# Cross attention: transposing the probabilities in 32x32 blocks on VectorE and moving the blocks by transfers within SBUF

## The chip, the cores and the metric

One core of a Trainium2 chip. Its engines work side by side, each through a queue of its own in order: TensorE (PE; its weight loads are shown as PEld), VectorE (DVE), ScalarE (ACT), GpSimd (POOL) and SyncE (SP), whose queue starts nearly all transfers; 16 DMA engines carry them out. The on-chip memory is SBUF (128 partitions); TensorE writes to PSUM, in banks of 128 x 512 floats. The metric is the time of one execution on the device in microseconds, as the median of the runs.

## The reference

One encoder layer over two sequences of 512 tokens of width 1024, each with a memory of 256 rows. Three branches (a state-space scan, a differential attention over the sequence, a cross attention to the memory) are gated, projected and summed, and a feed-forward block follows. All is float32. The part that the change touches is the cross attention, with 4 heads of 128:

```
def _cross_attention(q, mk, mv):
    Bn, L = q.shape[0], q.shape[1]
    s = jnp.einsum('blhd,bmhd->bhlm', q, mk).astype(jnp.float32) * (X_DH ** -0.5)
    probs = jax.nn.softmax(s, axis=-1).astype(mv.dtype)
    return jnp.einsum('bhlm,bmhd->blhd', probs, mv).reshape(Bn, L, X_WIDTH)
```

## The kernel before, in words

A matmul is made nearly exact in float32 by splitting each operand into a high part, rounded to the matmul's format, and a low part, the rest: three matmuls (high x high, high x low, low x high) for one product. The helper `split` (lines 134 and 135, or 137 and 138 with a scale) does it: ScalarE writes the high part, VectorE subtracts it from the source and writes the low part. All matmuls of the hand-ordered part go through `InOrder.matmul` and `InOrder.transpose` (lines 66 and 69), so in the profile they carry these two lines and are told apart by their tiles.

The cross attention is a loop (lines 686 to 726) over 32 steps: head h, sequence s, and a tile lt of 128 tokens, lt innermost; four steps with the same h and s are called a group here, and there are eight. For a step:

- scores: three matmuls of 128 tokens x 256 memory rows into a bank `sc`;
- softmax (`softmax_parts`, lines 541 to 550): VectorE takes the row maximum (`nb`), ScalarE the exponential `e` with the row sum, VectorE the reciprocal `r` and, on line 701, e times r;
- two steps later, TensorE transposes e in two pieces of 128x128 against the identity (line 69) into a bank `tr`, since the output matmul needs the memory rows on the partitions, and `split` brings the result from PSUM into `xpTh` and `xpTl`;
- after the fourth step of a group, six matmuls of 512 columns with the memory's values (`mvh`, `mvl`) give the outputs in a bank `oo`; ScalarE copies them to `xosb` (line 724) and SP stores them to `bD` (line 725).

TensorE's order in this part is the order of the program (`PE.on = True`); the other queues are ordered by the compiler's scheduler, with some edges given by hand (`tc.issue_after`). Between the parts of a step, `fill(n)` puts n units of other matmuls from `queue`: query projections of the next heads, gate tiles, the values of the next stage and its first projection, by `units` and `v_units`, one unit to a matmul of 512 columns. Their weights are loaded by `weight` (line 146) into a buffer `wf` of two, and split into `wh` and `wl`, of two each.

Each turn of the loop also ends in `half_piece`, which prepares weights of the last projection in the background: a load into `raw` (lines 443 and 445), sums on GpSimd (lines 452 to 455), a split into `hl` and a store to `wD` (line 472). These instructions are queued behind the last exponential (on ScalarE) and the last instruction of the softmax (on VectorE).

Two steps of scores run ahead (`AHEAD = 2`). The banks are 2 `mm` for projections, 3 `sc`, 2 `tr`, 1 `oo`. The pool `xT` has four buffers for `xpTh` and `xpTl`.

Of the kernel before, what the change touches and what calls it, by code (L numbers as in the profile page):

```python
# [10 lines left out]
F32 = mybir.dt.float32  # L11
F32R = mybir.dt.float32r
# [7 lines left out]
P = 128  # L20
L = 512
# [5 lines left out]
NMEM = 256  # L27
# [45 lines left out]
def encoder(ctx: ExitStack, tc: tile.TileContext, a, out):  # L73
    nc = tc.nc
    V, S, PO, PE = nc.vector, nc.scalar, nc.gpsimd, InOrder(tc, nc.tensor)
# [12 lines left out]
    def open_tags(es, side=None, **tags):  # L88

        for tag, n in tags.items():  # L90
            pools[tag] = es.enter_context(tc.tile_pool(name=tag, bufs=n, side=side, reuse_waits="tile"))

    def open_banks(**tags):

        bank_es.close()
        for tag, n in tags.items():
            pools[tag] = bank_es.enter_context(tc.tile_pool(name=tag, bufs=n, space=PSUM, reuse_waits="tile"))
# [4 lines left out]
    xp_es, phase = ExitStack(), ExitStack()  # L102
# [3 lines left out]
    def slot(tag, shape=(P, NT), dt=F32, name="sl"):  # L106
        return pools[tag].tile(list(shape), dt, tag=tag, name=name)

    def bank(tag="mm"):
        return pools[tag].tile([P, 512], F32, tag=tag, name="bk" + tag)  # L110

    def aux():
        return bank("tr")


    ident = cst.tile([P, P], F32, name="ident")
# [14 lines left out]
    def split(hi, lo, src, scale=None):  # L131

        if scale is None:
            h = S.copy(hi, src)  # L134
            l_ = V.tensor_tensor(out=lo, in0=src, in1=hi.bitcast(F32), op=ALU.subtract)  # L135
        else:
            h = S.activation(out=hi, in_=src, func=AF.Copy, scale=scale)
            l_ = V.scalar_tensor_tensor(out=lo, in0=src, scalar=scale, in1=hi.bitcast(F32), op0=ALU.mult, op1=ALU.subtract)
        return h, l_
# [55 lines left out]
    def factor(ss, n, nt=4, bias=epsc):  # L195

        rs = rp.tile([P, 4], F32, tag="rs", name="rs", bufs=4)
        S.activation(out=rs[:, :nt], in_=ss[:, :nt], func=AF.Sqrt, scale=1.0 / n, bias=bias)
        V.reciprocal(rs[:, :nt], rs[:, :nt])
        bc = aux()  # L200
        for t in range(nt):
            PE.transpose(bc[:, t * P : (t + 1) * P], rs[:, t : t + 1].broadcast_to([P, P]), ident)
        return rs, bc
# [144 lines left out]
    with yielding(last_s):  # L348
        x_norm(0, norm[0], range(5, 8))
        _, bc = factor(ss1, DM)  # L350
# [138 lines left out]
    def half_piece(behind_=()):  # L489
        with ExitStack() as es_:  # L490
            for i_ in behind_:
                es_.enter_context(tc.issue_after(i_.ins))
            return next(prep, None)
# [40 lines left out]
    last_x = None  # L534

    def softmax_parts(pool, col, sc, n, scale, nm, sums=None, bufs=2):


        nonlocal last_x
        nb = col.tile([P, 1], F32, tag=nm + "nb", name="nb")  # L540
        V.tensor_reduce(out=nb, in_=sc, axis=AX.X, op=ALU.max, negate=True)
        if scale != 1.0:
            V.tensor_scalar_mul(nb, nb, scale)  # L543
        e = pool.tile([P, n], F32, tag=nm + "e", name="e", bufs=bufs)
        sm = col.tile([P, 1], F32, tag=nm + "s", name="sm") if sums is None else sums
        last_x = S.activation(out=e, in_=sc, func=AF.Exp, bias=nb, scale=scale, accum_out=sm)
        if sums is not None:
            return e, sm
        r = col.tile([P, 1], F32, tag=nm + "r", name="r")
        V.reciprocal(r, sm)  # L550
        return e, r
# [28 lines left out]
    memory(1)  # L580

    open_banks(mm=2, sc=3, tr=2, oo=1)
    open_tags(phase, xT=4)
    xa = phase.enter_context(tc.tile_pool(name="xa", bufs=2, reuse_waits="tile"))
    xcol = phase.enter_context(tc.tile_pool(name="xcol", bufs=2, reuse_waits="tile"))

# [9 lines left out]
    def fill(n):  # L596
        nonlocal owed
        owed += n
        while owed > 0 and queue:
            r = next(queue[0], None)  # L600
            if r is None:
                queue.pop(0)
            else:
                owed -= r
        if not queue:
            owed = 0

    def finish(g):
        while any(g is g_ for g_ in queue):
            fill(1)  # L610
# [14 lines left out]
    def gate_units():  # L625
        t = next(todo)
        gt = slot("ld", name="gt")

        def use(s, o):
            S.activation(out=gt[:, s * L : (s + 1) * L], in_=o, func=AF.Tanh, scale=0.5)  # L630

        yield from units(a["w_in"][20 + t], xh, xl, use)
        nc.sync.dma_start(gD[t], gt)
# [37 lines left out]
        memory(3)  # L671
    lp = phase.enter_context(tc.tile_pool(name="lam", bufs=1, reuse_waits="tile"))

    lv = lp.tile([P, 4, 64], F32, tag="lv", name="lv", bufs=1)
    nc.sync.dma_start(lv, a["lamv"])
    V.tensor_tensor(out=lv[:, 0:2, :], in0=lv[:, 0:2, :], in1=lv[:, 2:4, :], op=ALU.mult)
    ld = lp.tile([P, 2], F32, tag="ld", name="ld", bufs=1)
# [6 lines left out]
    queue += [xq[1], gate_units(), xq[2], xq[3], v_units(0, v0), gate_units(), units(a["w_in"][4], xh, xl, dq0.__setitem__)]  # L684
    PE.on = True
    steps = [(h, s, lt) for h in range(4) for s in range(NS) for lt in range(4)]
    es, pT = {}, {}
    AHEAD = 2
    for i in range(-AHEAD, len(steps) + 1):
        if i + AHEAD < len(steps):  # L690
            h, s, lt = steps[i + AHEAD]
            if h and s == lt == 0:
                finish(xq[h])
            ms = slice(s * NMEM, (s + 1) * NMEM)
            qh, ql = (q_[:, lt * P : (lt + 1) * P] for q_ in qs[h, s])
            sc = bank("sc")
            PE.matmul(sc[:, :NMEM], qh, mkh[h][:, ms], start=True, stop=False)
            PE.matmul(sc[:, :NMEM], qh, mkl[h][:, ms], start=False, stop=False)
            PE.matmul(sc[:, :NMEM], ql, mkh[h][:, ms], start=False, stop=True)
            e, r = softmax_parts(xa, xcol, sc[:, :NMEM], NMEM, P ** -0.5, "x", bufs=3)  # L700
            last_e = last_x, V.tensor_scalar_mul(e, e, r)
            es[i + AHEAD] = e
        fill(9 if i == 0 else 5)
        if 0 <= i < len(steps):
            h, s, lt = steps[i]
            if lt == 0:
                pT[h, s] = tuple(slot("xT", [P, 2, L], F32R, n_) for n_ in ("xpTh", "xpTl"))
            e = es.pop(i)
            tr = aux()
            for j in range(2):  # L710
                PE.transpose(tr[:, j * P : (j + 1) * P], e[:, j * P : (j + 1) * P], ident)
            split(*(p_[:, :, lt * P : (lt + 1) * P] for p_ in pT[h, s]), tr[:, : 2 * P].rearrange("p (j q) -> p j q", j=2))
        fill(5 if i < len(steps) else 15)
        if i > 0 and steps[i - 1][2] == 3:
            h, s, _ = steps[i - 1]
            pTh, pTl = pT.pop((h, s))
            oo = bank("oo")
            hs = slice(h * P, (h + 1) * P)
            for j in range(2):
                PE.matmul(oo, mvh[s][:, j, hs], pTh[:, j, :], start=(j == 0), stop=False)  # L720
                PE.matmul(oo, mvh[s][:, j, hs], pTl[:, j, :], start=False, stop=False)
                PE.matmul(oo, mvl[s][:, j, hs], pTh[:, j, :], start=False, stop=(j == 1))
            osb = xa.tile([P, L], F32, tag="osb", name="xosb", bufs=1)
            S.copy(osb, oo)
            nc.sync.dma_start(bD[2, h, :, s * L : (s + 1) * L], osb)
        half_piece(last_e)
    while queue:
        fill(6)
    assert next(prep, None) is None
# [73 lines left out]
    def merges():  # L803
        res_.close()
        xp_es.close()
        open_tags(mes, side="right", mg=8, y=8)
        for m in range(KD):
            yield from merge_units(0, b0, m, first=True)
            if 3 <= m < 7:
                with tc.issue_after(last_s[0].ins):  # L810
                    merge_split(b2, 2, m - 3, "y", b2_in[m - 3])
            if 2 <= m < 6:
                b2_in.append(merge_load(2, m - 2))
        for m in range(KD):
            yield from merge_units(2, b2, m)
            if m == 2:
                open_tags(zes, side="right", z=4)
            if m in (2, 3):
                merge_split(b1, 1, m - 2, "z", merge_load(1, m - 2))
            elif m in (4, 5):  # L820
                b1_in.append(merge_load(1, m - 2))
# [8 lines left out]
    for _ in gate_units():  # L830
# [3 lines left out]
    queue += [qk_units(1, True), dk[1], gate_units(), qk_units(2, True), dk[2], v1_, qk_units(3, True), dk[3], gate_units(),  # L834
              gate_units(), merges()]
    s0, ss, osb = {}, {}, {}

    def scores(i):
        nonlocal last_e
# [66 lines left out]
    for i in range(-1, n + 3):  # L906
# [12 lines left out]
        if i in (17, 19, 21, 23):  # L919
            t = (0, 1, 3, 2)[(i - 17) // 2]  # L920
            with yielding(last_e):
                merge_split(b0, 0, t, "v" if t == 3 else "qk", first[t])
        if i in (15, 17, 19, 21):
            t = (0, 1, 3, 2)[(i - 15) // 2]
# [221 lines left out]
    for i in range(KFF):  # L1146
# [16 lines left out]
        if i == 0:  # L1163
            for s in range(NS):
                _, bc = rstd(accs[s], DM)
# [687 lines left out]
```

## Time and profile before

| | us |
|---|---|
| median of 3 runs | 1587.85 |
| lowest and highest run | 1587.73, 1587.97 |
| span of the profiled execution, first to last instruction | 1585.2 |
| the median less the span | 2.65 |
| TensorE busy in the span | 1574.0 |
| first and last transpose of the cross attention | 386.3, 486.2 |

The profiled execution is given by its span; what a run takes beyond the first and the last instruction is not in the trace. A row of a view names the line, the engine, the operation, the tile written and the tiles read (out<-in), and the shape. "Idle before" is the time for which the engine stood still just ahead of such an instruction, with what ended it. In the rows of one tile the three durations are the shortest, the median and the longest in ns; in the order of time the first two columns are the start and the duration in us.

### The profile page before, as it was taken

What the parts mean: (1) busy time and instruction counts of PE and PEld (TensorE: products, weight loads), DVE (VectorE), ACT (ScalarE), POOL (GpSimd) and SP (SyncE); (2) the same over time, 40 slices, a digit from 0 to 9 for tenths busy, and PEclk for the clock granted to TensorE, in tenths of its full rate; (3) what the DMA queues carried; (4) which work ended last, traced back from release to release, by engine and by line L of the source; (5) the groups of instructions that cost most, each with busy time, mean ns of one, the idle gap of its engine ahead of it and who ended that gap; (6) DMA issues with size and microseconds to landing.
All of it is one profiled execution on the core that took longest, in us unless ns stands there. A gap on an engine that the chain in (4) does not pass through costs nothing. (4 is left out here: it accounts for less than half of the span.)

```text
span 1585.2 us, 21351 instructions
## 1 busy us (share of the span) xinstructions
PE 1574.0 (99%) x7738; PEld 1310.4 (83%) x7738; DVE 1170.4 (74%) x1859; ACT 631.6 (40%) x1115; POOL 549.5 (35%) x434
## 2 busy tenths in 40 slices
PE   9999999999999999999999999999999999999998
PEld 7888888888898779778888888888888888888777
DVE  7978995076774776866545669788888877988864
ACT  6644223265552455564223443333333333233323
POOL 0010000001333321300343355767777553444663
PEclk9999999999999999999999999999999999999999
DMA  9553623676763121135544422333333323885412
GB/s 363 183 170 119 212 94 116 180 266 204 269 218 113 41 100 41 47 127 174 198 140 128 137 93 93 112 107 120 120 120 125 118 84 128 306 324 184 160 61 107
DMA packets 105675, 237.84 MB, mean 150 GB/s; under 512 B 13665, under 2 KB 45409, under 8 KB 105569
## 3 DMA queue, kind: packets, MB, share of 16 engines
q1 hardware_dynamic: 104992, 236.06, 44.2%
q8 instruction: 61, 1.00, 0.3%
q14 instruction: 46, 0.37, 0.1%
q10 hardware_dynamic: 576, 0.41, 0.1%
HBM read 165.16 MB, written 71.27 MB: 149 GB/s over the span
## 5 line engine op out<-in xcount | busy, mean ns | idle before, releaser
L66 PE MATMUL bkmm<-xh,wh 128*128 128x512 f32 x640 | 255.3, 399 | 0.0
L66 PE MATMUL bkmm<-xh,wl 128*128 128x512 f32 x640 | 250.6, 392 | 0.0
L66 PE MATMUL bkmm<-xl,wh 128*128 128x512 f32 x640 | 250.1, 391 | 0.0
L66 PE MATMUL bkmm<-tl,wh 128*128 128x512 f32 (+1 forms) x621 | 241.1, 388 | 0.0
L66 PE MATMUL bkmm<-th,wl 128*128 128x512 f32 (+1 forms) x621 | 240.7, 388 | 0.0
L66 PE MATMUL bkmm<-th,wh 128*128 128x512 f32 (+1 forms) x621 | 240.7, 388 | 0.0
L134 ACT CAST wh<-wf 128x1024 fp32r<-128x1024 f32 (+2 forms) x134 | 117.6, 878 | 261.2 <-PE bkmm L66 190.4
L135 DVE TENSOR_TENSOR wl<-wf,wh 128x1024 fp32r<-128x1024 f32 (+2 forms) x134 | 147.6, 1102 | 60.5 <-ACT wh L134 55.4
L66 PE MATMUL bkmm<-th,w 128*128 128x512 f32 x432 | 140.7, 391 | 1.9 <-DVE nsq L1112 1.2
L66 PEld LDWEIGHTS bkmm<-xh,wh 128*128 128x128 f32 x640 | 120.3, 188 | 26.2 <-issue 3.4
L66 PEld LDWEIGHTS bkmm<-xh,wl 128*128 128x128 f32 x640 | 120.2, 188 | 26.2 <-issue 0.4
L66 PEld LDWEIGHTS bkmm<-xl,wh 128*128 128x128 f32 x640 | 120.4, 188 | 22.3
L66 PEld LDWEIGHTS bkmm<-th,wh 128*128 128x128 f32 x621 | 116.6, 188 | 24.0
L66 PEld LDWEIGHTS bkmm<-th,wl 128*128 128x128 f32 x621 | 116.5, 188 | 24.1 <-DVE wl L135 0.2
L66 PEld LDWEIGHTS bkmm<-tl,wh 128*128 128x128 f32 x621 | 116.6, 188 | 23.8
L1175 POOL TENSOR_TENSOR up<-up,acc 128x512 f32<-128x512 f32 x44 | 83.7, 1920 | 90.6 <-DVE up L1112 86.8
L452 POOL TENSOR_TENSOR raw<-raw 128x128 f32<-128x128 f32 x28 | 14.6, 523 | 288.9 <-DVE nb L543 231.9
L66 PEld LDWEIGHTS bkmm<-th,w 128*128 128x128 f32 x432 | 80.9, 188 | 22.1 <-DVE nsq L1112 2.1
L792 POOL TENSOR_TENSOR mg<-mg,gl 128x1024 f32<-128x1024 f32 x16 | 43.8, 2740 | 136.8 <-DVE gl L788 132.1
L66 PE MATMUL bkmm<-tl,w 128*128 128x512 f32 x216 | 84.1, 389 | 0.0
L134 ACT CAST wh<-ws 128x1024 fp32r<-128x1024 f32 x44 | 46.3, 1052 | 91.3 <-PE bkmm L66 49.7
L66 PE MATMUL bkmm<-yh,wh 128*128 128x512 f32 x192 | 76.2, 397 | 0.0
(663 smaller groups left out, 3535.4 us busy)
## 6 DMA issues: line engine op xcount, KB each, us to landing
wf<-in_w_in SPq DMA_DIRECT2D x40, 512.0 KB, 3.9
wD<-hl SPq DMA_DIRECT2D x28, 512.0 KB, 2.9
w<-wD SPq DMA_DIRECT2D x28, 512.0 KB, 4.8
gD<-gt SPq DMA_DIRECT2D x24, 512.0 KB, 2.9
gl<-gD SPq DMA_DIRECT2D x24, 512.0 KB, 3.7
wf<-in_w_fg SPq DMA_DIRECT2D x22, 512.0 KB, 3.6
wf<-in_w_fu SPq DMA_DIRECT2D x22, 512.0 KB, 3.5
aD<-ac SPq DMA_DIRECT2D x22, 512.0 KB, 2.8
```

What stands on the lines that cost most here:

```text
L66: return self.put(self.eng.matmul(*args, **kw))
L134: h = S.copy(hi, src)
L135: l_ = V.tensor_tensor(out=lo, in0=src, in1=hi.bitcast(F32), op=ALU.subtract)
L452: PO.tensor_tensor(out=a22, in0=a21, in1=a22, op=ALU.add)
L792: PO.tensor_tensor(out=mg[m], in0=mg[m], in1=gt, op=ALU.add)
L1175: PO.tensor_tensor(out=up, in0=up, in1=accs[s], op=ALU.mult)
```

## The change

TensorE no longer transposes the probabilities. Right after the scaling, VectorE transposes e (128 tokens x 256 memory rows) in blocks of 32x32, into a tile `eT` that gathers the four steps of a group. A block transpose leaves each block in its own group of 32 partitions, so the blocks have to change partitions: after the fourth step, 16 transfers within SBUF (one for each pair of a source group g and a target group c of 32 partitions, 32 KB each in runs of 512 bytes) bring them to the tile `xr`, all on SP's queue. Two turns later than before, one `split` of 128x1024 for the whole group makes the high part in `xT`, now one buffer, and the low part in place in `xr`, two buffers. The output matmuls come one turn after it. The columns of `xr` are in another order, which the copy from `oo` to `xosb` puts right. The loop has two turns more at its end; `half_piece` runs as often as before. There are two buffers for e in place of three, and the small vector `lv` takes a buffer of the pool `ld`.

```diff
-    open_tags(phase, xT=4)
+    open_tags(phase, xT=1, xr=2)
...
-    lv = lp.tile([P, 4, 64], F32, tag="lv", name="lv", bufs=1)
+    lv = slot("ld", [P, 4, 64], name="lv")
...
-    for i in range(-AHEAD, len(steps) + 1):
+    for i in range(-AHEAD, len(steps) + 3):
...
-            e, r = softmax_parts(xa, xcol, sc[:, :NMEM], NMEM, P ** -0.5, "x", bufs=3)
-            last_e = last_x, V.tensor_scalar_mul(e, e, r)
-            es[i + AHEAD] = e
+            e, r = softmax_parts(xa, xcol, sc[:, :NMEM], NMEM, P ** -0.5, "x", bufs=2)
+            V.tensor_scalar_mul(e, e, r)
+            if lt == 0:
+                xe[h, s] = xa.tile([P, 8, 4, 32], F32, tag="eT", name="eT", bufs=2)
+            last_e = last_x, V.transpose(xe[h, s][:, :, lt, :], e)
+            if lt == 3:
+                raw = xr_[h, s] = slot("xr", [P, 2, L], F32R, "xpTl")
+                rows = xe.pop((h, s)).rearrange("p (j c) t q -> p j c (t q)", c=4)
+                for g in range(4):
+                    for c in range(4):
+                        nc.sync.dma_start(raw.bitcast(F32)[32 * c : 32 * c + 32, :, P * g : P * g + P], rows[32 * g : 32 * g + 32, :, c])
         fill(9 if i == 0 else 5)
-        if 0 <= i < len(steps):
-            h, s, lt = steps[i]
-            if lt == 0:
-                pT[h, s] = tuple(slot("xT", [P, 2, L], F32R, n_) for n_ in ("xpTh", "xpTl"))
-            e = es.pop(i)
-            tr = aux()
-            for j in range(2):
-                PE.transpose(tr[:, j * P : (j + 1) * P], e[:, j * P : (j + 1) * P], ident)
-            split(*(p_[:, :, lt * P : (lt + 1) * P] for p_ in pT[h, s]), tr[:, : 2 * P].rearrange("p (j q) -> p j q", j=2))
-        fill(5 if i < len(steps) else 15)
-        if i > 0 and steps[i - 1][2] == 3:
-            h, s, _ = steps[i - 1]
+        if 4 <= i < len(steps) + 2 and steps[i - 2][2] == 3:
+            h, s, _ = steps[i - 2]
+            lo, hi = xr_.pop((h, s)), slot("xT", [P, 2, L], F32R, "xpTh")
+            split(hi, lo, lo.bitcast(F32))
+            pT[h, s] = hi, lo
+        fill(5)
+        if i > 4 and steps[i - 3][2] == 3:
+            h, s, _ = steps[i - 3]
...
-            S.copy(osb, oo)
+            S.copy(osb.rearrange("p (t g q) -> p g t q", t=4, q=32), oo.rearrange("p (g t q) -> p g t q", t=4, q=32))
...
-        half_piece(last_e)
+        if i <= len(steps):
+            half_piece(last_e)
```

More of the change, by code (lines that the diff above doesn't have):

```diff
@@ L686, in encoder @@
     steps = [(h, s, lt) for h in range(4) for s in range(NS) for lt in range(4)]
-    es, pT = {}, {}
+    pT, xe, xr_ = {}, {}, {}
     AHEAD = 2
-    for i in range(-AHEAD, len(steps) + 1):
+    for i in range(-AHEAD, len(steps) + 3):
         if i + AHEAD < len(steps):
@@ L836, in encoder @@
     s0, ss, osb = {}, {}, {}
+    es = {}
     def scores(i):
```

## The prediction

> **What bounds the kernel now.** I read the page first, then the busy time by stretch, then the instructions in order of time around one cross-attention step.
>
> ```profile
> span 1585.2 us, 21351 instructions
> PE 1574.0 (99%) x7738; PEld 1310.4 (83%) x7738; DVE 1170.4 (74%) x1859; ACT 631.6 (40%) x1115; POOL 549.5 (35%) x434
> ```
>
> ```profile
> core 0: us, PE busy (x) PEld busy (x) DVE busy (x) ACT busy (x) POOL busy (x), PEclk, DMA share, GB/s
> 386.00:488.00 102.00, 102.00 (x612) 89.31 (x611) 73.73 (x201) 59.32 (x150) 31.17 (x62) 1.00 0.66 231
> ```
>
> The second fence is the stretch that holds the 32 cross-attention steps. TensorE is busy for all of its 102.00 us at full clock (1.00), so in this stage time is what TensorE's queue takes, and its order is written out by hand. VectorE has 28.3 us free there, ScalarE 42.7, the DMA engines a third. What TensorE no longer does is gained in full, as long as nothing in its fixed order has to wait for what replaces it.
>
> The 1585.2 us are the span of the profiled execution; the median of the runs, 1587.85 us, is 2.65 us more. The sum below is made on the span, and the 2.65 us stay as they are.
>
> **What leaves TensorE.** The price of a transpose is not its duration but how far it pushes the next matmul:
>
> ```profile
> 423.50 0.39 PE L66 MATMUL bkmm<-xh,wl 128*128 128x512 f32 x1
> 423.73 0.38 PE L69 MATMUL bktr<-ident,e 128*128 128x128 f32 x2
> 423.87 0.48 PE L66 MATMUL bkmm<-xh,wh 128*128 128x512 f32 x1
> 424.18 0.39 PE L66 MATMUL bkmm<-xl,wh 128*128 128x512 f32 x1
> 424.41 0.39 PE L66 MATMUL bkmm<-xh,wl 128*128 128x512 f32 x1
> ```
>
> ```profile
> L69 PE MATMUL bktr<-ident,e x64: 270/271/276, 386.3 to 486.2; 128*128 128x128 f32 x64
> L134 ACT CAST xpTh<-bktr x32: 355/373/385, 386.7 to 486.5; 128x256 fp32r<-128x256 f32 x32
> L135 DVE TENSOR_TENSOR xpTl<-bktr,xpTh x32: 406/418/425, 387.1 to 486.9; 128x256 fp32r<-128x256 f32 x32
> ```
>
> Matmuls of 512 columns start 0.23 us apart (424.18 to 424.41). From the pair of transposes to the second matmul behind it are 0.45 us (423.73 to 424.18), so the pair costs 0.22 us. There are 64 transposes, 32 pairs: 32 x 0.22 = 7.0 us leave the path. (The durations would say 64 x 0.271 = 17.3 us; they overlap, so I don't use them.) The Trainium skill, VectorE: DVE Perf Modes, The three transpose paths, puts a 128x128 transpose at 390 ns on TensorE and 311 ns on VectorE (bf16); by its figure 64 of them would give an estimated 25 us back. The trace does not agree, and the sum goes by the cadence.
>
> **VectorE and ScalarE.** The 32 casts (0.373 us) and subtractions (0.418 us) from PSUM become eight of each over 128x1024 from SBUF, and 32 block transposes of 128x256 come. Nearest rows:
>
> ```profile
> L135 DVE TENSOR_TENSOR wl<-wf,wh 128x1024 fp32r<-128x1024 f32 x8 | 10.0, 1255 | 2.7 <-ACT wh L134 2.5
> L134 ACT CAST wh<-wf 128x1024 fp32r<-128x1024 f32 x7 | 7.3, 1045 | 1.2 <-PE bkmm L66 1.1
> L752 DVE STREAM_SHUFFLE t<-bkmm 128x512 f32<-128x512 f32 x1 | 0.7, 734 | 0.0
> L701 DVE TENSOR_SCALAR e<-e,r 128x256 f32<-128x256 f32 x32 | 12.7, 397 | 0.9
> ```
>
> No block transpose is in this trace. It lies between half the shuffle of 512 columns (0.37) and the whole of it (0.73); with an instruction's fixed part the subtraction of the same 256 columns, 0.42, is nearest in size, and I take 0.45. VectorE: 73.7 - 32 x 0.418 + 8 x 1.255 + 32 x 0.45 = 84.8 us, in a stage that shrinks to 95: 89% busy. At 0.73 it would be 93.7, 99%. ScalarE: 59.3 - 11.9 + 8.4 = 55.8. The output copy now reads its columns in another order; were each of its eight 1 us longer, ScalarE would still have 31 us free. So neither is the bound, but VectorE's queue gets long waits. The exponentials' buffers (three, now two) cost nothing: the transpose follows the scaling directly and frees one about 5 us before it is wanted.
>
> **The queue of SP.** Each group of four steps (one head of one sequence, eight groups) adds 16 transfers of 32 KB, 128 in all, on the queue that carries the weights, the prepared pieces of the last projection (raw, hl) and the outputs. Bursts of small transfers are in the trace elsewhere:
>
> ```profile
> 297.17 3.65 SPq L1753 DMA_DIRECT2D yD<-y__2854  x8
> 113.15 4.78 SPq L1674 DMA_DIRECT2D u__1192<-uD  x9
> 394.81 0.33 SPq L472 DMA_DIRECT2D wD<-hl  x1
> 395.23 0.39 SPq L443 DMA_DIRECT2D raw<-in_w_fo  x1
> 395.67 0.78 SPq L445 DMA_DIRECT2D raw<-in_w_fo  x1
> 396.54 4.60 SPq L472 DMA_DIRECT2D wD<-hl  x2
> ```
>
> ```profile
> wD<-hl SPq DMA_DIRECT2D x16, 512.0 KB, 3.0
> wD<-hl SPq DMA_DIRECT2D x16, 384.0 KB, 3.2
> wf<-in_w_in SPq DMA_DIRECT2D x6, 512.0 KB, 3.6
> raw<-in_w_fo SPq DMA_DIRECT2D x24, 128.0 KB, 3.3
> bD<-xosb SPq DMA_DIRECT2D x8, 256.0 KB, 3.3
> wf<-in_w_v SPq DMA_DIRECT2D x2, 512.0 KB, 4.2
> gD<-gt SPq DMA_DIRECT2D x2, 512.0 KB, 2.8
> ```
>
> A transfer in a burst takes 3.65/8 = 0.46 us of SP, or 4.78/9 = 0.53; I take 0.46, from the burst that nothing interrupts. A group's 16 take 7.3 us (8.5 at 0.53). The others of the stage, by the spacing of the rows: 50 of 0.42 (32 hl, 8 outputs, 8 weights, 2 gates), 12 pairs of raw at 0.44 + 0.87: 21.0 + 15.7 = 36.7 us. With 128 x 0.46 = 58.9 that is 95.6 us of issuing in a stage of 95. SP goes from a third to full. That is the danger of this change.
>
> The Trainium skill, DMA: Bandwidth & Descriptors, Issuing engines are not separate DMA queues, calls the time to start a transfer "usually small relative to the DMA itself". For these bursts the trace does not agree: eight take 3.65 us to issue and land 2.0 us after issue. By that rule the transfers would cost nothing and the full 7.0 us would stay, 1580.8.
>
> The DMA engines themselves have room:
>
> ```profile
> yD<-y__2854 SPq DMA_DIRECT2D x8, 64.0 KB, 2.0
> q1 hardware_dynamic: 875, 0.40, 47.4%
> q1 hardware_dynamic: 12088, 24.99, 62.1%
> DMA to landing us min/median/max: 1.9/3.2/7.5
> ```
>
> The first two rows and the last are the yD stores, the second in a window of 4 us; the third is the 115 us from 380 to 495. 875 packets of some 460 bytes took 0.474 x 16 x 4 = 30 us, 35 ns each. The 128 transfers make 8192 packets of 512 bytes: 287 us over 16 engines, 18 us each of 115, so the share goes from 62% to 78%.
>
> **The chain that TensorE can wait for.** Scores, softmax, transpose, transfers, cast and subtraction, then the output matmuls; in the new order five steps lie between a group's last scores and its outputs.
>
> ```profile
> 426.72 0.28 PE L66 MATMUL bksc<-mkvh,qh 128*128 128x256 f32 x1
> 428.78 0.35 DVE L701 TENSOR_SCALAR e<-e,r 128x256 f32<-128x256 f32 x1
> 442.08 0.36 PE L66 MATMUL bksc<-mkvh,qh 128*128 128x256 f32 x1
> ```
>
> 426.72 are the scores of step 15, a group's last, 442.08 those of step 20. Behind these come 0.35 us of scores and ten units of projection (2.3 us), and five pairs of transposes (1.1 us) go: 15.4 + 2.7 - 1.1 = 17.0 us of cover. The chain: 2.4 us to the scaled exponentials (428.78 + 0.35 - 426.72), 0.5 transpose, 15 x 0.46 = 6.9 to the last issue, 2.0 to 3.2 to land, 1.05 cast, 1.26 subtraction, some 0.6 between engines: 14.7 to 15.9 us. So it fits with 1 to 2 us to spare, which one busy moment of VectorE or another group's transfer in the burst uses up. A stall at one output also lengthens the cover of the next group, whose last scores lie before it, so about half of an excess is paid. I allow a loss of 2 us over the eight groups, ends 0 and 13 (below).
>
> Weights don't suffer:
>
> ```profile
> 393.61 0.33 SPq L146 DMA_DIRECT2D wf<-in_w_v  x1
> 407.72 1.03 ACT L134 CAST wh<-wf 128x1024 fp32r<-128x1024 f32 x1
> 422.07 1.04 ACT L134 CAST wh<-wf 128x1024 fp32r<-128x1024 f32 x1
> ```
>
> With two buffers the load of 393.61 is for the second cast behind it, 422.07: 28 us ahead, more than a burst. The two steps added to the loop hold no work but projection units that the loop behind it ran before; the vector lv moved to a buffer of a pool in use is one small load before the stage. Both at nothing.
>
> Sum: 1585.2 - 7.0 + 2.0 = 1580.2 of span, with 2.65 around it 1582.8 us.
>
> **The rivals.** (1) The transfers land late. At 0.53 an issue, 3.2 to land and 1 us more in VectorE's queue the chain is 2.4 + 0.5 + 8.0 + 3.2 + 1.05 + 1.26 + 1.6 = 18.0 against 17.0, and with softmax 2 us later 20.0: an excess of 1 to 3 us, half of it paid, eight times: 4 to 13 us back, or 1585 to 1594; the middle of what I think likely, 6 us, is 1586.8, no change to be told. For it: the cover is so tight. Against: softmax runs 2.4 us in the step shown.
>
> (2) SP becomes the bound, and the kernel is slower. Now the stage takes 99.9 us from the first transpose to the last, 31 steps, so 12.9 us for a group. While raw pieces are loaded SP needs for a group 7.3 to 8.5 for the blocks and about 5.5 for the rest, 12.8 to 14.0, and the burst stands at the head of the queue until VectorE is done. An hl store behind a burst is 7 us late; the next cast of hl then waits for its buffer in ScalarE's queue, and behind it the exponentials and the copies that free TensorE's banks. It happens a little already:
>
> ```profile
> ACT hl L137 <- DMA wD<-hl: 2.4, 2, 1.5
> ```
>
> It decides from 12.9 us of SP per group on. At 14.0 and eight groups TensorE loses 8 x 1.1 = 9 us against now: 1597. For it: the 95.6 us of issuing. Against: raw and hl can fall behind for a while, and the last three groups have no raw loads. Batching to 1 MiB is the rule of the Trainium skill, DMA: Bandwidth & Descriptors (Measured), which calls transfers under 64 KB descriptor-dominated; the bursts of 64 KB above agree, and the change goes against it.
>
> **How the numbers follow.** A measurement here can tell about 0.2%, 3.2 us, from no change. Forecast, 1580.8 to 1584.7: 0.50. Rival 1, of which the worst is slower: 0.24, of it 0.20 same and 0.04 slower. Rival 2: 0.26, of it 0.02 same and 0.24 slower. Faster 0.50, same 0.22, slower 0.28. The range goes from 1580.3 (the full gain and 0.5 us of rounding in the 0.22) to 1595, which leaves out most of rival 2 and little else.
>
> **What would show it.** Right: no transposes of e by TensorE in the stage, TensorE still without gaps, the stage 5 to 7 us shorter, block transposes near 0.45 us, bursts on SP near 7.3 us, a few us of waits of the output matmuls for the subtraction of the low part. Rival 1 shows as such waits above 4 us in all; rival 2 as ScalarE's hl casts waiting for their stores, and TensorE waiting for banks. A gain above 7.5 us, or the lost time outside this stage, would make the reasoning wrong.

## The result, and the profile after

The changed kernel takes 1633.56 us (median of 5 runs, 1631.94 to 1634.76), the kernel before 1587.73 on the same chip (5 runs). The ratio is 1.0289, 95% interval 1.0276 to 1.0301: 46 us slower. The forecast was 1582.8, with a range to 1595.0.

First the head of the page of after (its profiled execution):

```profile
span 1630.2 us, 21386 instructions
PE 1581.5 (97%) x7674; PEld 1311.9 (80%) x7674; DVE 1180.0 (72%) x1867; ACT 630.8 (39%) x1091; POOL 546.2 (34%) x434
```

The span is 45.0 us longer. TensorE has 64 instructions fewer and yet 7.5 us more of busy time, and stands still for 48.7 us in place of 11.2. It is not work that was added to TensorE. The 40 slices of the page say where it happens; the busy tenths of PE and the granted clock of after:

```profile
PE   9999999999768899999999999999999999999998
PEclk9999999999879999999999999999999999999999
```

Slices of 40.8 us: apart from the very last, only the 11th to 14th differ from 9, the stretch from about 408 to 570 us, and in the first two of these the granted clock falls too. The first scores of the next stage start at 519.0 before and at 563.7 after, 44.7 us later, so nearly the whole loss is made in the cross attention. The same stretch in pieces of 20 us (columns as in the prediction):

```profile
core 0: us, PE busy (x) PEld busy (x) DVE busy (x) ACT busy (x) POOL busy (x), PEclk, DMA share, GB/s
400.00:420.00 20.00, 15.51 (x63) 12.35 (x62) 11.12 (x31) 8.83 (x19) 5.37 (x12) 0.83 0.50 157
...
440.00:460.00 20.00, 8.49 (x30) 6.36 (x30) 8.09 (x17) 5.93 (x11) 3.66 (x8) 0.67 0.61 206
460.00:480.00 20.00, 13.04 (x88) 12.49 (x89) 10.09 (x23) 7.52 (x15) 3.65 (x8) 0.74 0.60 205
480.00:500.00 20.00, 19.76 (x154) 18.90 (x152) 14.30 (x39) 9.74 (x23) 4.60 (x8) 1.00 0.50 167
```

From 440 to 460 us no column of work is near full: TensorE is busy 8.5 of 20 us, VectorE 8.1, the DMA engines 0.61 of the time. Everybody waits. For what, TensorE's queue shows in order of time (the brackets: idle time before, and what ended it):

```profile
408.39 0.49 PE L66 MATMUL bkoo<-xpTh,mkvh 128*128 128x512 f32 x1 [3.32 <-ACT xpTh L134]
...
442.32 0.79 PE L66 MATMUL bkoo<-xpTh,mkvh 128*128 128x512 f32 x1 [5.33 <-ACT xpTh L134]
...
466.28 0.58 PE L66 MATMUL bkmm<-wh,xh 128*128 128x256 f32 x1 [15.00 <-ACT wh L134]
...
535.28 0.73 PE L66 MATMUL bkoo<-xpTh,mkvh 128*128 128x512 f32 x1 [4.60 <-ACT xpTh L134]
```

Two kinds of wait: outputs for the high part of their probabilities, and, the longest, a projection unit for the split of its weights. Behind both stands one queue. SP in the same trace, in order of time (start, duration of the issuing, count):

```profile
393.70 0.42 SPq L443 DMA_DIRECT2D raw<-in_w_fo  x1
394.17 0.71 SPq L445 DMA_DIRECT2D raw<-in_w_fo  x1
394.98 0.51 SPq L472 DMA_DIRECT2D wD<-hl  x1
395.60 10.35 SPq L710 DMA_DIRECT2D xpTl<-eT  x16
406.05 0.53 SPq L472 DMA_DIRECT2D wD<-hl  x1
...
445.28 2.51 SPq L710 DMA_DIRECT2D xpTl<-eT  x4
447.89 0.53 SPq L472 DMA_DIRECT2D wD<-hl  x1
448.47 7.63 SPq L710 DMA_DIRECT2D xpTl<-eT  x12
...
458.67 0.98 SPq L472 DMA_DIRECT2D wD<-hl  x2
459.70 1.70 SPq L146 DMA_DIRECT2D wf<-in_w_v  x2
```

Row follows on row: from 393.70 to 462 us there is no pause above 0.42 us. A burst of 16 takes 10.35 us, 0.65 us a transfer. From the first burst (395.60) to the start of the fourth (445.28) three groups take 49.7 us, 16.6 each, where the rest of the stage would take TensorE some 12 (the 102 us of before, less 7, by eight). The loads of the value weights stand behind four bursts: their buffer is free from about 396.5 on (the low part of the weights in it begins at 395.31 and takes 1.2 us), the load is issued at 459.70. Before, the same loads were issued at 393.61 and 410.05. Their place in the queue has changed too: counted from 360 us on, one pair of `raw` loads and three stores of `hl` stood ahead of the first of them before, nine pairs, 18 stores and 64 block transfers after. The tile of the transposed blocks, with shortest, median and longest duration in ns:

```profile
L710 SPq DMA_DIRECT2D xpTl<-eT x128: 585/595/1290, 395.6 to 532.2; - x128
L704 DVE STREAM_TRANSPOSE eT<-e x32: 397/445/447, 388.4 to 520.2; 128x256 f32<-128x256 f32 x32
DMA to landing us min/median/max: 1.8/1.9/5.9
```

The third row is the landing: 1.9 us after issue. The transfers are quick and their issue is slow.

### The profile page after: what moved, and what is told of

Read it like the earlier page. It is cut to its first block, busy times and chain, and to the rows that moved or that the text cites. A ratio compares the mean times of both kernels' runs of the same rounds, so it can differ in the third digit from the quotient of the medians.

```text
span 1630.2 us, 21386 instructions
## 1 busy us (share of the span) xinstructions
PE 1581.5 (97%) x7674; PEld 1311.9 (80%) x7674; DVE 1180.0 (72%) x1867; ACT 630.8 (39%) x1091; POOL 546.2 (34%) x434
## 5 line engine op out<-in xcount | busy, mean ns | idle before, releaser
L66 PEld LDWEIGHTS bkmm<-xl,wh 128*128 128x128 f32 x640 | 121.4, 190 | 23.1
```

Source lines behind the costliest of these rows:

```text
L66: return self.put(self.eng.matmul(*args, **kw))
```

## The experiments

Theory A: SP's queue is the bound; 16 issues a group are too many, and what stands behind them (weights, stores) comes late. Rival B: the chain from the scores to the split is too long for the five steps that cover it; a later output would cure that. Rival C: VectorE, with its block transposes, is the late one. Rival D, stated after the first three runs: with the queue relieved, the traffic itself (landings, stores that hold ScalarE) still costs. The kernel before took 1587.6 to 1588.2 us in all four sets.

**lag2: outputs two steps later.** The edit:

```diff
-    for i in range(-AHEAD, len(steps) + 3):
+    for i in range(-AHEAD, len(steps) + 5):
...
-        if 4 <= i < len(steps) + 2 and steps[i - 2][2] == 3:
+        if 6 <= i < len(steps) + 4 and steps[i - 4][2] == 3:
...
-        if i > 4 and steps[i - 3][2] == 3:
+        if i > 6 and steps[i - 5][2] == 3:
```

> The changed kernel with the split and the output matmuls of a group two steps later (5.3 us more of TensorE's work between the scores and the outputs). Theory A (SP's queue is full: a transfer takes 0.65 us of SP, 16 take 10.4, with 5.5 for the rest 15.9 us per group where TensorE needs 12): more cover doesn't help a full queue, 1622 to 1636 us. Rival B (the chain is merely 3 to 5 us longer than its cover): the waits of the output matmuls go, 1583 to 1595 us. Rival C (VectorE and ScalarE stand still behind the large split in their queues): the split comes later, part of the loss goes, 1600 to 1620.

Measured: 1636.17 us (one run), as A has it. Of the 21.2 us that TensorE waits ahead of output matmuls in after, 9.0 went, and the waits for weights took them up, 30.8 us in place of 15.7. TensorE's two largest rows in the waits (total, times, longest):

```profile
PE bkmm L66 <- ACT wh L134: 30.1, 2, 28.1
PE bkoo L66 <- ACT xpTh L134: 9.2, 3, 4.2
```

Two steps more of cover bought nothing, so B, which had 1583 to 1595, falls as the main cause.

**runs1k: the same 16 transfers, with runs of 1 KB.** A transposed tile in another order, so that each transfer is 32 runs of 1 KB in place of 64 of 512 bytes:

```diff
-                xe[h, s] = xa.tile([P, 8, 4, 32], F32, tag="eT", name="eT", bufs=2)
+                xe[h, s] = xa.tile([P, 4, 2, 4, 32], F32, tag="eT", name="eT", bufs=2)
...
-                        nc.sync.dma_start(raw.bitcast(F32)[32 * c : 32 * c + 32, :, P * g : P * g + P], rows[32 * g : 32 * g + 32, :, c])
+                        nc.sync.dma_start(raw.bitcast(F32)[32 * c : 32 * c + 32, g].rearrange("p j x -> p (j x)"), rows[32 * g : 32 * g + 32, c])
```

> The changed kernel with the same 16 transfers of 32 KB, each of 32 runs of 1 KB in place of 64 of 512 bytes, and with plain two-dimensional patterns on both sides. Theory A, if the issue time lies in the pattern or the number of runs: issues of 0.33 to 0.45 us, 16 in 5.5 to 7.5 us, 1590 to 1612 us. Theory A, if the issue time is fixed for such a transfer within SBUF: 0.58 to 0.6 us as now, 1628 to 1636. Rivals B and C don't look at the issue time; B would follow the length of the burst alone.

Measured: 1631.19 us (one run), and the rows of eT say why:

```profile
L710 SPq DMA_DIRECT2D xpTl<-eT x128: 507/589/1435, 394.5 to 531.7; - x128
```

589 ns for half the runs against 595: the price is that of one transfer and does not follow the number of its runs.

**dram5: five transfers a group by way of device memory.**

```diff
-                for g in range(4):
-                    for c in range(4):
-                        nc.sync.dma_start(raw.bitcast(F32)[32 * c : 32 * c + 32, :, P * g : P * g + P], rows[32 * g : 32 * g + 32, :, c])
+                xd = drp.tile([4, 32, 2, 4, P], F32, name=f"xD{h}_{s}")
+                for g in range(4):
+                    nc.sync.dma_start(xd[:, :, :, g].rearrange("c r j x -> r j c x"), rows[32 * g : 32 * g + 32])
+                nc.sync.dma_start(raw.bitcast(F32), xd.rearrange("c r j g x -> (c r) j (g x)"))
```

> The changed kernel with the blocks moved by way of device memory: four stores of 128 KB (one for each source group of 32 partitions) and one load of 512 KB for each group of steps, in place of 16 transfers within SBUF. VectorE's and ScalarE's work is as in the changed kernel. Theory A: 5 issues of 0.4 to 0.65 us are 2 to 3.3 us of SP per group, SP has room again, and what TensorE saved shows: 1580 to 1586 us. Rival B: the chain is 2.4 + 0.5 + 2.5 + 3 + 4 + 1.05 + 1.26 + 1 = 15.7 us, hardly shorter than with the 16 transfers (16 to 18), so waits of the outputs stay: 1590 to 1615. Rival C: nothing changes for these two engines, 1615 or more.

Measured: 1603.82 us (4 runs), ratio 1.0101 (1.0084 to 1.0118). The bytes move twice, and 30 of the 46 us are back. The weight loads are issued at 398.21 and 412.93 again, and TensorE has no wait for weights. What is left are four waits of outputs of 0.7 to 4.3 us, with 0.5 to 0.8 more behind each one's first matmul: two landings, 3.8 and 4.9 us in the median, now stand in the chain. So what A says of the weights holds, but A's time, 1580 to 1586, does not. The time and the kind of wait that is left are those that B had for this run (1590 to 1615): with the queue relieved, the chain is too long for its cover.

**dram5_lag2: both.** The edits of lag2 and dram5 together.

> The two edits of dram5 and lag2 together: blocks by way of device memory in five transfers, split and outputs two steps later. In dram5 SP had room again, and the 13.3 us that TensorE stood still were all before the outputs, 0.7 to 4.3 us each, with the transfers landing in 4 to 5 us. Theory A (a full queue, and behind it a chain that is a little too long): with both mended the waits go and the 7.0 us of the transposes stay: 1580 to 1584 us. Rival C (VectorE, 12 us more to do, holds the stage): 1592 or more. Rival D (the device-memory traffic, DMA share 0.9, delays more than the outputs): 1588 to 1600.

Measured: 1596.12 us (5 runs), ratio 1.0054 (1.0040 to 1.0067). The longest waits that are left are one of 4.29 us for the high part and one of 2.53 for a VectorE split of the queries. A's 1580 to 1584 are missed. The time lies where D has it, with the hl stores landing after 5.0 to 5.6 us (3.0 to 3.2 before) at a DMA share of 0.85 to 0.96 from 400 to 500 us, and also where C has it (1592 or more). Which of these made the two waits was not taken apart.

**Other queues for part of the issues.** half_gpsimd sends half of the 16 from GpSimd's queue, quarter_act a quarter from ScalarE's; weights_act leaves the 16 on SP and sends the weight loads of the stage from ScalarE's:

```diff
-                        nc.sync.dma_start(raw
+                        (nc.sync if c % 2 else nc.gpsimd).dma_start(raw
```

```diff
-                        nc.sync.dma_start(raw
+                        (nc.scalar if c == 3 else nc.sync).dma_start(raw
```

```diff
-        last_w = nc.sync.dma_start(wf[:, :n], src)
+        last_w = (nc.scalar if on_act else nc.sync).dma_start(wf[:, :n], src)
```

> The changed kernel with 8 of a group's 16 transfers started from GpSimd's queue. Theory A: SP needs 8 x 0.65 + 5.5 = 10.7 us of a group's 12, its queue has room, the weights are loaded ahead again: 1585 to 1605 us. Rival C: no change, above 1620. If starting a transfer costs GpSimd over 1.5 us, its 8 take 12 us beside its other work and the time is above 1605 for that reason.

> The changed kernel with 4 of a group's 16 transfers started from ScalarE's queue. Theory A: SP needs 12 x 0.65 + 5.5 = 13.3 us per group in place of 15.9, 21 us less in all, still over 12: 1602 to 1616 us, if ScalarE bears 4 x 0.65 = 2.6 us more of its own and the wait for the transposes. Rival C: no gain, 1630 or more, since ScalarE is behind.

> The changed kernel with the ten weight loads of the stage started from ScalarE's queue, the bursts on SP as they are. In the changed kernel the value weights were loaded at 459.7 us, 63 us after their buffer came free, and TensorE stood still for 15.7 us. Theory A': SP's order has pushed the prefetch behind four groups of bursts; freed of that the 15.7 us and some slow clock behind them go, and the waits for the outputs stay or grow by some us: 1606 to 1620 us. If the rate of SP alone sets the time, whatever is late: 1626 to 1634, as the outputs take up the wait.

Measured, one run each: half_gpsimd 1611.35, quarter_act 1623.13, weights_act 1622.52. The first two are 6 and 7 us above the ranges that A had given them, the third lies between its two ranges. The more of the issues SP loses, the more comes back: 22 us for 64 of the 128, 10 for 32. On GpSimd an issue takes 536 ns in the median, on ScalarE 607. In half_gpsimd no weight comes late, in quarter_act one wait of 13.0 us for weights stays. weights_act is the telling one: its weight wait of 15 us is gone, yet only 11 us come back. TensorE still waits ahead of the outputs, 23.1 us in all against 21.2 in after (its two largest rows; in after they are 17.0, 5, 5.3 and 2.9, 4, 1.2), and is slow for another 17.2 us (14.1 in after; counted as in the section on the prediction below):

```profile
PE bkoo L66 <- ACT xpTh L134: 16.0, 6, 4.0
PE bkoo L66 <- DVE xpTl L135: 5.5, 6, 1.3
```

SP still needs its time for a group: from 395.8 to 522.5 us its queue has no pause above 0.7 us in this run, and its eight bursts start 16.5 us apart on the average (395.8 to 511.5). Against TensorE's 12 that is 36 us in eight groups, of the 41 by which the run is above the version without transfers (below). So of the 46 us some 11 are the late place of the weight loads in the queue's order, and the pace of the queue is most of the rest. A further version, with 12 of the 16 transfers and GpSimd copying the four blocks that stay on their partitions, has no measured time.

**no_transfers: the transfers left out.** The split reads eT directly:

```diff
-                raw = xr_[h, s] = slot("xr", [P, 2, L], F32R, "xpTl")
-                rows = xe.pop((h, s)).rearrange("p (j c) t q -> p j c (t q)", c=4)
-                for g in range(4):
-                    for c in range(4):
-                        nc.sync.dma_start(raw.bitcast(F32)[32 * c : 32 * c + 32, :, P * g : P * g + P], rows[32 * g : 32 * g + 32, :, c])
+                xr_[h, s] = xe.pop((h, s))
...
-            lo, hi = xr_.pop((h, s)), slot("xT", [P, 2, L], F32R, "xpTh")
-            split(hi, lo, lo.bitcast(F32))
+            lo, hi = slot("xr", [P, 2, L], F32R, "xpTl"), slot("xT", [P, 2, L], F32R, "xpTh")
+            split(*(t_.rearrange("p j x -> p (j x)") for t_ in (hi, lo)), xr_.pop((h, s)).rearrange("p a t q -> p (a t q)"))
```

> The changed kernel without the 16 transfers: the split reads the gathered block transposes as they are. It leaves out the blocks' way between partitions, so its output is not the reference's; all the work of TensorE, VectorE and ScalarE is that of the changed kernel. Theory A (the loss comes from the transfers alone): TensorE's 7.0 us show, 1579.5 to 1583 us. Rival C (VectorE's 32 block transposes and large subtractions cost too): 1586 us or more.

Measured: 1581.67 us (5 runs), ratio 0.9962 (0.9948 to 0.9976): 6.0 us faster than before. The stretch that the prediction showed for before:

```profile
386.00:488.00 102.00, 101.65 (x579) 89.25 (x578) 83.28 (x218) 57.73 (x129) 39.09 (x66) 1.00 0.69 242
```

VectorE does all its new work, 83.28 us of 102, and TensorE stands still for 0.35. C falls as the cause of the loss: the block transposes fit.

**transfers_unread: the same, with the 16 transfers back on SP, into a tile that nobody reads.** (The pool `xT` has two buffers here and `xr` one.)

```diff
+                raw = slot("xr", [P, 2, L], F32R, "raw")
+                rows = xr_[h, s].rearrange("p (j c) t q -> p j c (t q)", c=4)
+                for g in range(4):
+                    for c in range(4):
+                        nc.sync.dma_start(raw.bitcast(F32)[32 * c : 32 * c + 32, :, P * g : P * g + P], rows[32 * g : 32 * g + 32, :, c])
```

> As no_transfers, with the 16 transfers of a group issued on SP as in the changed kernel, into a tile that nothing reads. It leaves out the same part of the computation. Theory A (SP's queue is full, and what stands behind the bursts is late): weights and prepared pieces are late though no output waits for a transfer, 1605 to 1630 us. Rival B (the loss is the outputs' wait for the blocks): near no_transfers, 1579 to 1588.

Measured: 1634.89 us (one run), 5 us above A's range and far from B's. No instruction reads what these transfers bring (the block transposes wait 2.9 us in all for a buffer that is still being read), and 53 us come all the same. TensorE's two waits of any size:

```profile
467.36 0.58 PE L66 MATMUL bkmm<-wh,xh 128*128 128x256 f32 x1 [31.96 <-ACT wh L134]
...
540.29 0.79 PE L66 MATMUL bkmm<-xh,wh 128*128 128x512 f32 x1 [13.84 <-ACT wh L134]
```

Both are for weights, whose loads SP issues at 460.90 and 533.65, each behind four bursts. This settles it for A: the time goes into SP's queue, by what stands behind the bursts, and not into waiting for the blocks. In after a part of the same delay is met at the outputs, and the wait for weights is shorter.

**half_gpsimd_lag2, half_groups, half_groups_dram: what a mended version gives.** The first joins two edits above. half_groups makes block transposes for the groups of the second sequence alone (64 transfers on SP), the others by TensorE as before; half_groups_dram does that with the five transfers of dram5. Their core:

```diff
+            if s == 0:
+                es[i + AHEAD] = e
+            else:
...
+        if 0 <= i < len(steps) and steps[i][1] == 0:
...
+                PE.transpose(tr[:, j * P : (j + 1) * P], e[:, j * P : (j + 1) * P], ident)
```

> half_gpsimd with the split and the outputs two steps later. SP has 10.7 us of issuing in a group's 12 and nearly all of the 18 us that TensorE stood still in half_gpsimd was before the outputs. Theory A: with more cover that goes, and with it the slow clock behind each wait: 1583 to 1593 us. If the DMA engines or GpSimd's own queue hold it: 1596 to 1608.

> Only the four groups of the second sequence go by block transposes and 16 transfers on SP; those of the first are transposed by TensorE as in the kernel before. Theory A: two groups need 16 x 0.65 + 2 x 5.5 = 21.4 us of SP and 24.7 of TensorE, so the queue has room on average: of the 46 us lost nearly all goes, by more than half; TensorE saves 3.5 us; a burst of 10.4 us still delays what stands behind it, 0 to 2 us in each of four: 1584 to 1593 us. If the loss went with the number of transfers, half of it would stay: 1607 to 1612.

> half_groups with the blocks by way of device memory in five transfers. SP needs 3.3 + 11 = 14.3 us of two groups' 24.7 and its longest burst is 2.7 us. Theory A: what TensorE saves in four groups shows, 3.5 us less 0 to 2 of late outputs: 1584 to 1587 us. Rival D (device-memory traffic): 1588 to 1594.

Measured: half_gpsimd_lag2 1605.69 us (4 runs), ratio 1.0113 (1.0098 to 1.0129); half_groups 1605.70 (4 runs), 1.0113 (1.0099 to 1.0127); half_groups_dram 1595.82 (5 runs), 1.0053 (1.0039 to 1.0066). All three are above the ranges that A had given them. half_groups lies next to the 1607 to 1612 of a loss in proportion to the number of transfers, though SP has room there (67 us of issuing in the 98 us between its first and its last block transfer); half_groups_dram is above D's 1594 as well. half_gpsimd_lag2 has one wait of 3.46 us for an output and one of 9.05 at the start of the next stage, for VectorE. half_groups waits at each of its four block groups (1.5 to 3.3 us, and 0.6 to 0.9 behind the first matmul), and half_groups_dram at three (one of 2.2 us the longest).

The wait of 9.05 us in half_gpsimd_lag2 can be followed. SP stands 7.5 us at a weight load whose buffer is not yet free (until 503.00), and the hl stores behind it come late. ScalarE's next cast of hl waits 5.25 us for one (508.48), and VectorE's subtraction waits for that cast. Behind it in VectorE's queue stand the operations on `t` (until 511.21) that TensorE waits for at 511.26.

No version that moves the blocks beats the kernel before.

## Why the prediction was wrong

**The step that failed is the price of an issue, and with it the sum for SP.** The prediction took 0.46 us from a burst of stores into device memory. The transfers within SBUF take 0.65 (10.35 / 16; 0.595 of it the instruction), with runs of 512 bytes as with runs of 1 KB. In the three groups above, 48 block transfers take 31.7 us (10.35 + 2.92 + 8.31 + 2.51 + 7.62), 10.6 a group, and the rest of SP's work 18.0, 6.0 a group: 16.6, where the prediction had 12.8 to 14.0. The sum for the time holds nothing for SP's queue, and that was wrong by the prediction's own figures: after the gain TensorE needs 12.0 a group, so 12.8 to 14.0 would cost 0.8 to 2.0, or 4 to 10 us in the five groups with raw loads, of a gain of 7.0. It compared them with 12.9, the group before the gain, and put "SP goes from a third to full" into a rival with 0.26. Rival 2 had the right mechanism, SP as the bound, and a fifth of its size: its 1597 is 9 us above before, 1.1 us a group, and 46 were measured.

**"Weights don't suffer" failed.** It looked at a lead of 28 us and one burst, and took the queue's order as it was. In after the load comes behind four bursts and 15 more stores of hl, 63 us after its buffer was free, and TensorE waited 15.0 and 0.68 us there. The scheduler made that order; with fewer issues on SP (no_transfers, dram5, half_gpsimd) the load is early again, behind three or four stores. What made the scheduler change it, no run shows. The prediction named late hl stores as what would hold ScalarE; they grew too (waits of ScalarE for them from 2.4 to 15.9 us in all), but TensorE was not held by them first.

**The transfers that land late** (rival 1) were the wrong end of the chain: landing is 1.9 us, below the 2.0 to 3.2 taken. The chain is long by its burst: 10.35 us of issuing, where 15 x 0.46 = 6.9 to the last issue were taken. The Trainium skill, DMA: Bandwidth & Descriptors, Issuing engines are not separate DMA queues, calls the issue "usually small relative to the DMA itself"; the traces disagree for these transfers, with 0.65 us each, 10.35 for 16 in a row, against 1.9. By that sentence the time would have been near the 1581.67 of no_transfers.

**Right:** the transposes' price on TensorE, 7.0 us (no_transfers gains 6.0, and from its first scores to those of the next stage it takes 133.7 us in place of 140.7); the block transpose, 0.445 us for 0.45; the casts and subtractions of 1024 columns, 1.046 and 1.226 us for 1.045 and 1.255; the output copy in another order at nothing (586 ns against 587 before, in the median); VectorE and ScalarE not the bound; and the room on the DMA engines.

**Where the loss lies.** From the first scores of the cross attention to the first of the next stage after takes 184.7 us (378.96 to 563.66), no_transfers 133.7 (378.84 to 512.57), with the same matmuls: 288 of 256 columns and 434 of 512. At the spacing of an undisturbed TensorE, 0.119 and 0.228 us, these take 133.2. What is above that is in after 37.4 us of standing still and 14.1 of a slow TensorE, in no_transfers 0.35 and 0.2. So of the 51 us between the two, over a quarter is no waiting at all but a slow TensorE; of that more below. The same for dram5_lag2: 150.0 us, of it 10.7 standing still and 6.1 slow, 16.3 above no_transfers, as are the spans (1596.1 and 1579.8).

**Open:** what makes most of the 7 to 16 us of waits that stay in the last three versions and in dram5_lag2. The wait of 9.05 us above goes by the path that rival 2 had named, late hl stores that hold ScalarE; for the others the rows name landings, a split of queries on VectorE and stores, at a DMA share of 0.85 to 0.96 (dram5_lag2) and 0.73 to 0.85 (half_groups_dram) in the stretches looked at; no run takes one of these away.

## What to carry to other kernels

Before work is moved from a busy engine to transfers, add up the issuing of every queue for one group of the loop, at the price of that very kind of transfer, and compare it with the time that the loop is to take after the gain, not before. A queue that is over that sets the pace of the loop (16.5 us a group in weights_act, against 12), and a load that was far ahead can come to stand behind its bursts; so the order of the queue is to be read again after the change. And a version with the transfers kept but unread, beside one without them, tells in two runs whether the data or the queue is what costs.

## What the runs showed of the hardware beyond that

A short rest of TensorE costs more than itself. After the wait of 15.0 us the matmuls of 256 columns start 0.21 us apart, and only later 0.12, as the granted clock is 0.50 from 466.3 to 470.5 us and 1.00 from there. TensorE in after, in order of time:

```profile
466.28 0.58 PE L66 MATMUL bkmm<-wh,xh 128*128 128x256 f32 x1 [15.00 <-ACT wh L134]
467.54 0.58 PE L66 MATMUL bkmm<-wl,xh 128*128 128x256 f32 x1 [0.68 <-DVE wl L135]
467.92 0.41 PE L66 MATMUL bkmm<-wh,xl 128*128 128x256 f32 x1
468.13 0.41 PE L66 MATMUL bkmm<-wh,xh 128*128 128x256 f32 x1
...
470.48 0.31 PE L66 MATMUL bksc<-mkvh,ql 128*128 128x256 f32 x1
470.63 0.28 PE L66 MATMUL bkmm<-wh,xh 128*128 128x256 f32 x1
470.75 0.28 PE L66 MATMUL bkmm<-wl,xh 128*128 128x256 f32 x1
```

From 466.28 to about 470.5 it runs at little more than half its pace, some 2 us lost. The price does not follow the length of the rest: it is 1.9 us behind the wait of 31.96 us in transfers_unread and 3.2 behind the 13.84 us of the same run, 2.0 behind a pair of 2.21 and 0.76 in half_groups and 3.1 behind one of 3.32 and 1.17 in after. Nor does the total of a pair decide whether there is a price. A pair of 1.53 and 0.77 us in half_groups leaves the pace as it was:

```profile
420.50 0.49 PE L66 MATMUL bkoo<-xpTh,mkvh 128*128 128x512 f32 x1 [1.53 <-ACT xpTh L134]
421.76 0.50 PE L66 MATMUL bkoo<-xpTl,mkvh 128*128 128x512 f32 x1 [0.77 <-DVE xpTl L135]
422.10 0.39 PE L66 MATMUL bkoo<-xpTh,mkvl 128*128 128x512 f32 x1
422.33 0.39 PE L66 MATMUL bkoo<-xpTh,mkvh 128*128 128x512 f32 x1
```

while a shorter one of 0.71 and 0.76 us in dram5 (at 466.12 and 467.38) halves the clock behind it. The difference is where the rest falls. The changes of the granted clock lie multiples of 3.41 us apart in each of these profiles. Cut on that grid, dram5 has both its rests in one stretch, half_groups one in each of two (columns as above, the granted clock third from the end; dram5, then half_groups):

```profile
464.30:467.70 3.40, 1.93 (x12) 1.40 (x11) 1.60 (x3) 2.03 (x4) 0.00 (x0) 1.00 1.04 380
467.70:471.10 3.40, 3.40 (x13) 2.98 (x12) 2.07 (x6) 1.19 (x3) 1.56 (x4) 0.50 0.89 295
```

```profile
416.60:420.00 3.40, 2.37 (x12) 1.59 (x10) 0.19 (x2) 0.59 (x1) 0.00 (x0) 1.00 0.40 143
420.00:423.40 3.40, 2.13 (x10) 1.60 (x11) 2.33 (x5) 1.58 (x5) 0.00 (x0) 1.00 1.01 357
423.40:426.80 3.40, 3.40 (x20) 2.84 (x19) 2.49 (x9) 2.77 (x8) 1.85 (x4) 1.00 1.10 308
```

The same count over the twelve profiles that have transfers, from 370 to 560 us, takes the stretches of 3.41 us at full clock in which TensorE stands still for over 0.25 us: behind the 40 with up to 1.43 us the next stretch has the full clock, behind the 44 with 1.68 or more it has half, and of the four between, from 1.47 to 1.64, one is followed by half. The Trainium skill, TensorE: Matmul & The Clock Gate, Why this matters for your kernels, advises against rests of more than about 3 us between bursts of matmuls, since the clock falls to half. The traces agree for rests of that length, but rests of half of it, alone or summed, are enough where they fall into one stretch. So in an otherwise gapless kernel a rest of about 1.6 us or more is to be priced at itself plus one or two stretches at half pace, an estimate of 1.7 to 3.4 us, unless it falls across the border of two.
